# Attention sums kept as channels x tokens up to the output projection, their denominators inverted by way of DRAM, and the two output norms applied to the products

## The chip, the cores and the metric

One core of a Trainium2 chip runs the whole layer in one launch. The metric is the device time of that launch in microseconds (us). A core has a matrix engine (PE), a vector engine (DVE), a scalar engine (ACT), a general engine (POOL), and queues that issue transfers (DMA); here nearly all transfers are issued by SP, in order. SBUF is the on-chip memory, PSUM the eight accumulation banks that PE writes, DRAM the memory behind the DMAs.

## The reference

One encoder layer over 1024 tokens of width 1024, in float32:

```python
hn = rms_norm(x, norm1_g)
qa, ka, va, qb, kb, vb = split(hn @ w_in)              # A: 8 q heads, 2 kv heads; B: 8 heads; 64 channels each
out_a = softmax(rope(norm(qa)) @ rope(norm(ka)).T / 8) @ va          # dense, 4 q heads to a kv head
out_b = mixture of three dilated windows over norm(qb), norm(kb), vb # one sum over 3 patterns, one denominator
mixed = concatenate([rms_norm(out_a, outa_norm_g), rms_norm(out_b, outb_norm_g)], -1)   # 512 + 512 columns
x = x + mixed @ w_out                                  # 1024 x 1024
x = x + conv_ffn(rms_norm(x, norm2_g), w_up, conv_w, conv_b, w_down) # gate/value, width-3 conv, gelu
```

`rms_norm(y, g) = y * rsqrt(mean(y*y) + 1e-6) * g`, over the last axis.

## The kernel before

**Data.** All of SBUF is two arenas: `bigf` (float32) and `bigr` (the form that PE takes at its fast rate). A float32 product is made of three fast matmuls: a value is split into a high part (a copy into `bigr`) and a low part (value minus high part), and high x high, high x low and low x high are summed in a PSUM bank (`ps`). A copy by ACT and a subtraction by DVE make one split. A PE transpose of a `bigf` tile needs no split; in the profile it is a MATMUL `ps<-bigf`.

**Order of the work.** The code calls engine methods through a `Recorder`. It keeps every operation, works out dependences, and a planner (`price`, `simulate`) places them: PE's operations carry their place in the code as priority, those of the other engines a latest start worked out from prices; `emit` then writes each engine's queue in that planned order. So each engine runs its instructions in a fixed order, every instruction has the same source line (L462 before, L467 after the change, as order prints them), and an instruction that waits holds up whatever stands behind it on its engine. A DMA on SP also waits for the DMA eight before it, whose semaphore it shares.

**Stages.** Input projections and their norms; attention A in 16 groups `g` (128 tokens `b`, kv head `kv`; four q heads are one 512-wide tile); attention B, 8 heads of 8 steps `s` with a lag of two steps between scores (`b_s`) and sums (`b_pv`); output projection, residual and second norm; the feed-forward's two products.

**Attention A** (`a_main`). For each of 8 key tiles `kt`: scores on PE, two exponentials on ACT (one to `bigr` as the high part `ph`, one in place in PSUM), DVE subtracts them to the low part `pl`; three matmuls (`pv`) add value x probability into a bank, three key tiles behind. The bank holds 64 channels x 512 (4 heads x 128 tokens), and row 64 the denominators. `o_out` (ACT) copies the 65 rows to SBUF. `o_turn` then turns them back with four PE transposes of 65 rows, and `o_norm` (DVE) takes the reciprocal of 4 denominators per token and multiplies: tokens x channels, into the q tile that is no longer needed. The tail of a group (`pv(5..7)`, `o_out`, `o_turn`) runs inside the next.

**Attention B** (`b_pv`, `b_out`). The sums for 512 tokens (`hf` 0 or 1) lie as 65 x 512 in banks 6 and 7; the last matmuls of a head (steps 4 to 7) have the float32 weight `F_VCN` (65 columns) and appear as `ps<-bigf 128*65`. `b_out` turns and divides as in A, one step later.

**Output projection.** `x` tiles run in the order `seq(i)`. `mix_norm(i, u)` takes the RMS of 512 columns (u = 0: A, u = 1: B): an ACT square with a sum, DVE, an ACT square root, four DVE operations (`newton`), one DVE product with scale and gain. `mix_tr(i, u)` transposes the 128 x 512 result with four PE transposes, and `evac_split` makes the split operand from PSUM. `proj_out(i, u, hf)` is 12 matmuls of 512 columns, both `u` into one bank of a ring of six (`pj`). `h2_a` adds the residual, squares, norms; `h2_b` transposes for the feed-forward. `wo_load`/`wo_split` load and split the eight 128-row blocks of `w_out` through three buffers `F_WOR`; the first blocks are split in B's last head (`mixer_out_early`), which also does `mix_norm` for two tiles. `wu_load` loads `w_up` into four buffers, two of which are `F_WOR`'s.

Of the kernel before, what the change touches and what calls it, by code (L numbers as in the profile page):

```python
# [129 lines left out]
class Recorder:  # L130
# [335 lines left out]
def tile_encoder_layer(ctx, tc, x, xt, w_kv, w_in, gains, outg, norm2_g, w_out, w_up, conv,  # L466
# [471 lines left out]
    def a_main(g, prep, tail, late, plan, late_plan):  # L938
# [38 lines left out]
        return [lambda: pv(5), lambda: pv(6), lambda: pv(7), o_out, o_turn]  # L977

    def o_norm(t, step, dst, dims):
        rec = f(SM_T + 88 + 8 * (t % 2), 4)  # L980
        vec.reciprocal(rec, pp(512 * t + 64, [step, 4]))
        vec.tensor_tensor(fp(dst, *dims), pp(512 * t, [step, 4], [1, 64]), rec[:, :, None].to_broadcast([128, 4, 64]),
                          op=OP.mult)


# [190 lines left out]
    def x_load(i):  # L1176
        dma(f(F_X + 1024 * (i % 2), 1024), perm_rows(x, seq(i), D))

    def mix_norm(i, u):
        t = SM_T + 16 * (i % 2) + 8 * u  # L1180
        o = fp(q_at(1 - u, seq(i), 0), [512, 2], [1, 256])
        act(heads(f(F_JK3, 256).bitcast(BF), 2), o, AF.Square, accum_out=f(t, 1))
        vec.tensor_scalar(f(t + 1, 1), f(t, 1), 1.0 / 512, EPS, op0=OP.mult, op1=OP.add)
        act(f(t + 2, 1), f(t + 1, 1), AF.Sqrt)
        newton(f(t + 3, 1), f(t + 1, 1), f(t + 2, 1), f(t + 4, 1))
        vec.scalar_tensor_tensor(o, o, f(t + 3, 1), heads(f(F_OG + 512 * u, 512), 2), op0=OP.mult, op1=OP.mult)

    def mix_tr(i, u):
        b = next_tr()
        for k in range(4):  # L1190
            tr_f(b, k, f(q_at(1 - u, seq(i), k // 2) + 128 * (k % 2), 128))
        evac_split(xs(i) + 512 * u, b)

    def pj(i, hf):
# [607 lines left out]
```

## Time and profile before

| | us |
|---|---|
| median of 3 runs (1270.86 to 1271.05) | 1270.92 |
| the profiled execution | 1271.11 |
| its span (first to last instruction) | 1269.3 |
| TensorE clock granted, mean of the span | 1.0 of full speed |

The stages in that span: input projections to about 177 us (with the preparation of A), A to about 407, B to about 539, output projection to about 645, feed-forward to the end. In the profile a row of groups reads: engine, operation, out<-in with sizes, xcount, busy time, mean ns of one, and what ended the idle time before. A matmul's own duration includes its way through the array, so the rate is read from the distance between starts. A row of the timeline is: start, duration, engine, operation, count, and in brackets idle time and its releaser.

### The profile page before, as it was taken

The page shows a single profiled execution, that of the slowest core. Times are in us where ns is not written, and L with a number is a line of the kernel's source. Part 1 is how long each engine was busy: PE and PEld are TensorE (multiplying, and loading weights), DVE is VectorE, ACT ScalarE, POOL GpSimd, SP SyncE. Part 2 cuts the span into 40 slices and gives each one's busy share as a digit, 9 for nine tenths or more (in the row PEclk, how much of TensorE's full clock was granted, in tenths as well). Part 3 has the DMA queues.
Part 4 walks back from the last instruction along what each step waited for, and adds up shares of the span by engine and source line. Part 5 has one row for each costly group of instructions (what it writes and reads, how often), then busy time and mean ns, then how long its engine had stood idle before and what let it go on. Part 6 is the DMA issues. An engine that isn't in the chain of part 4 may idle for free.

```text
span 1269.3 us, 17891 instructions
## 1 busy us (share of the span) xinstructions
PE 1255.4 (99%) x6244; PEld 1048.8 (83%) x6244; DVE 1078.7 (85%) x1940; ACT 745.9 (59%) x1222; POOL 88.9 (7%) x92
## 2 busy tenths in 40 slices
PE   7999999999999999999999999999999999999998
PEld 7888887888888999778888888888888888888887
DVE  5988889999887888886699989999999998876664
ACT  6876479988888777763455444444444455344331
POOL 0011230020002221001120000000000000000000
PEclk9999999999999999999999999999999999999999
DMA  9242341000005445442321322333322248977862
GB/s 358 73 161 67 83 126 40 13 1 10 1 18 138 121 115 131 127 163 85 108 74 51 125 94 89 100 108 108 125 93 90 100 148 285 325 257 234 283 228 104
DMA packets 118777, 157.43 MB, mean 124 GB/s; under 512 B 50720, under 2 KB 75808, under 8 KB 117664
## 3 DMA queue, kind: packets, MB, share of 16 engines
q1 hardware_dynamic: 117392, 152.88, 37.2%
q0 software_dynamic: 1152, 3.15, 0.9%
q8 instruction: 49, 0.80, 0.3%
q10 hardware_dynamic: 144, 0.27, 0.1%
q14 instruction: 40, 0.33, 0.1%
HBM read 118.26 MB, written 33.82 MB: 120 GB/s over the span
## 4 chain that ended last, share of the span: by engine, by line
PE 93%; DVE 3%; ACT 2%; issue 1%; DMA 1%; POOL 1%; DVEq 0%; ACTq 0%; POOLq 0%
PE ps L462 93%; DVE bigf L462 2%; DVE bigr L462 1%; ACT bigr L462 1%; POOL bigf L462 0%; DMA bigf<-w_out 0%; DMA bigf<-w_kv 0%; ACT bigf L462 0%; ACT L462 0%; ACT ps L462 0%; POOL bigr L462 0%; DVEq L462 0%; ACTq L462 0%; POOLq L462 0%
## 5 line engine op out<-in xcount | busy, mean ns | idle before, releaser
L462 PE MATMUL ps<-bigr 128*128 128x512 f32 (+3 forms) x5860 | 1226.1, 369 | 8.5 <-ACT bigr L462 7.5
L462 PEld LDWEIGHTS ps<-bigr 128*128 128x128 f32 x5860 | 1010.3, 186 | 202.6 <-ACT bigr L462 11.7
L462 ACT ACTIVATE bigr<-bigf 128x512 fp32r<-128x512 f32 (+2 forms) x388 | 276.8, 727 | 350.6 <-PE ps L462 284.7
L462 DVE TENSOR_TENSOR bigr<-bigf,bigr 128x512 fp32r<-128x512 f32 (+2 forms) x354 | 283.4, 813 | 62.9 <-ACT bigr L462 58.9
L462 DVE TENSOR_TENSOR bigf<-bigf 128x512 f32<-128x512 f32 (+3 forms) x308 | 213.7, 718 | 24.0 <-DMA bigf<-w_down 12.5
L462 DVE TENSOR_TENSOR bigf<-ps,bigf 128x512 f32<-128x512 f32 (+3 forms) x260 | 174.8, 681 | 40.5 <-PE ps L462 35.1
L462 ACT ACTIVATE bigr<-ps 128x512 fp32r<-128x512 f32 x292 | 166.6, 602 | 68.7 <-PE ps L462 64.7
L462 ACT ACTIVATE bigf<-bigf 128x1024 f32<-128x1024 f32 (+6 forms) x194 | 152.1, 804 | 43.3 <-DVE bigf L462 29.0
L462 DVE SCALAR_TENSOR_TENSOR bigf<-bigf 128x255 f32<-128x255 f32 (+5 forms) x283 | 161.6, 591 | 5.3 <-ACT bigf L462 2.5
L462 DVE TENSOR_TENSOR bigr<-ps,bigr 128x512 fp32r<-128x512 f32 x188 | 127.4, 685 | 31.2 <-ACT ps L462 22.1
L462 ACT ACTIVATE ps<-ps 128x512 f32<-128x512 f32 x192 | 115.0, 600 | 12.6 <-PE ps L462 11.6
L462 ACT ACTIVATE bigf<-ps 128x512 f32<-128x512 f32 (+3 forms) x112 | 70.2, 634 | 27.5 <-DVE bigf L462 13.7
L462 DVE TENSOR_REDUCE bigf<-ps 128x1 f32<-128x512 f32 x128 | 81.5, 681 | 0.9 <-PE ps L462 0.8
L462 PE MATMUL ps<-bigf 65*128 65x65 f32 (+2 forms) x384 | 63.2, 293 | 1.3 <-DVE bigf L462 1.3
L462 POOL TENSOR_TENSOR bigr<-bigf,bigr 128x512 fp32r<-128x512 f32 x32 | 41.8, 1311 | 313.4 <-ACT bigr L462 185.8
L462 PEld LDWEIGHTS ps<-bigf 65*128 65x128 f32 (+2 forms) x384 | 43.7, 139 | 13.3 <-DVE bigf L462 2.3
L462 POOL TENSOR_TENSOR bigf<-bigf 128x256 f32<-128x256 f32 (+2 forms) x29 | 34.3, 1205 | 193.8 <-DVE bigf L462 187.4
L462 DVE CUSTOM_DVE_ANT_1 bigf<-ps,bigf 128x432 bf16<-128x432 f32 x64 | 38.5, 602 | 4.2 <-PE ps L462 2.8
L462 DVE CUSTOM_DVE_ANT_0 bigf<-ps,bigf 128x256 bf16<-128x256 f32 x64 | 26.8, 419 | 1.2 <-PE ps L462 1.2
L462 DVE TENSOR_REDUCE bigf<-bigf 128x16 f32<-128x1024 f32 x13 | 15.8, 1215 | 0.5 <-ACT bigf L462 0.5
L462 ACT ACT_TABLE_LOAD x11 | 14.1, 1283 | 1.4 <-PEq L1794 1.2
L462 POOL MEMSET bigr<- 64x512 f32 (+2 forms) x18 | 8.1, 478 | 40.3 <-PE ps L462 40.2
(17 smaller groups left out, 50.6 us busy)
## 6 DMA issues: line engine op xcount, KB each, us to landing
bigf<-w_down SPq DMA_DIRECT2D x99, 256.0 KB, 3.9
bigf<-w_up SPq DMA_DIRECT2D x44, 512.0 KB, 3.5
bigf<-gscr SPq DMA_DIRECT2D x77, 256.0 KB, 4.0
gscr<-bigf SPq DMA_DIRECT2D x33, 512.0 KB, 2.9
bigf<-w_in SPq DMA_DIRECT2D x8, 1024.0 KB, 6.8
bigf<-x SPq DMA_DIRECT2D x16, 512.0 KB, 4.6
bigf<-tmx SPq DMA_DIRECT2D x8, 672.0 KB, 4.4
bigr<-bigr SPq DMA_DIRECT2D x16, 256.0 KB, 3.3
```

Of the source, the lines that this page charges most:

```text
L462: method(*args, **kw)
```

## The change

- **A.** `o_turn` and `o_norm` go. After `o_out` two DMAs move the sums to the q tile as channels x tokens (two heads on the 128 partitions), and one DMA writes the row of 512 denominators to DRAM (`dscr`). After each second group, `inverse` reads 1024 denominators back as 128 x 8, DVE inverts them, a DMA writes them, and two DMAs read them back repeated over 64 partitions each (`F_RB`). POOL multiplies the sums by them and forms the sum of squares over the heads (`F_SS`, 128 partitions x tokens).
- For two of the eight key tiles (`kt` 0 and 4) the second exponential goes to SBUF and POOL makes `pl` from it, not DVE.
- **B.** The same with `b_out`, called from `b_pv`; `inverse` after each second head, for `hf` 0 and 1. The squares of the last pair of heads are made by ACT, the others by POOL.
- **Output projection.** No transposes of attention outputs: `mix_split` splits them in place. Instead four `square_sums` (each four PE transposes of `F_SS` and a DVE reduction) give the sums of squares per token, `mix_rms` the two roots for all 8 tiles at once. The gain goes into the rows of `w_out` in `wo_split`; the RMS factor is applied to the product in `proj_add`, so u = 0 and u = 1 have banks of their own and two additions to the residual. Three `x` buffers, not two.
- The planner's price of a reciprocal changes from `n / 0.96 + 92` to `6.2 n + 68`.

```diff
@@ Recorder.price
             if name == "reciprocal":
-                t += 24
+                t = 6.2 * n + 68
@@ a_main
         def o_out():
-            act(f(F_OT[g % 2], 512)[0:65], bank(ob)[0:65], AF.Copy)
-
-        def o_turn():
-            t = next_tr()
-            for i in range(4):
-                pe.transpose(bank(t, 65, 128 * i), f(F_OT[g % 2] + 128 * i, 128)[0:65], f(O_IDF, 65)[0:65])
-            o_norm(t, 128, q_at(1, b, kv), ([64, 4], [1, 64]))
+            o = F_OT[g % 2]
+            act(f(o, 512)[0:65], bank(ob)[0:65], AF.Copy)
+            for u in range(2):
+                dma(fp(q_at(1, b, kv), [128, 2], [1, 128])[64 * u:64 * u + 64],
+                    fp(o + 128 * u, [256, 2], [1, 128])[0:64])
+            dma(d_ap(0, b, 512 * kv, [512, 1], [1, 512]), f(o, 512)[64:65])
+            if kv:
+                inverse(b, [[0, 64], [256, 4], [1, 128]], 128)
+                o, sq = fp(q_at(1, b, 0), [512, 2], [1, 256]), F_SQ
+                gp.tensor_tensor(o, o, heads(f(F_RB, 512), 2), op=OP.mult)
+                gp.tensor_tensor(heads(f(sq, 512), 2), o, o, op=OP.mult)
...
-            act(bank(st), bank(st), AF.Exp)
-            vec.tensor_tensor(r(pl, 512), bank(st), rf(ph, 512), op=OP.subtract)
+            if kt in (0, 4) and True:
+                act(f(p, 512), bank(st), AF.Exp)
+                gp.tensor_tensor(r(pl, 512), f(p, 512), rf(ph, 512), op=OP.subtract)
+            else:
+                act(bank(st), bank(st), AF.Exp)
+                vec.tensor_tensor(r(pl, 512), bank(st), rf(ph, 512), op=OP.subtract)
...
+    def inverse(n, dims, step):
+        d = f(F_D8 + 8 * (n % 2), 8)
+        dma(d, d_ap(0, n, 0, [8, 128], [1, 8]))
+        vec.reciprocal(d, d)
+        dma(d_ap(1, n, 0, [8, 128], [1, 8]), d)
+        for u in range(2):
+            dma(f(F_RB, 512)[64 * u:64 * u + 64], d_ap(1, n, step * u, *dims))
+
+    def square_sums(u, hf):
+        t = next_tr()
+        for i in range(4):
+            tr_f(t, i, f(F_SS + 512 * hf + 128 * i, 128))
+        vec.tensor_reduce(f(F_RMS + 8 * u + 4 * hf, 4), heads(bank(t), 4), axis=AX.X, op=OP.add)
@@ b_pv, b_out
-            vec.tensor_tensor(o[0:65], bank(6 + hf)[0:65], o[0:65], op=OP.add)
+            vec.tensor_tensor(f(F_OD[hf], 512)[0:65], bank(6 + hf)[0:65], o[0:65], op=OP.add)
+            b_out(h, hf)
...
+        dma(x[64 * u:64 * u + 64], heads(f(F_OD[hf], 512), 4)[0:64])
+        dma(d_ap(0, n, 512 * u, [512, 1], [1, 512]), f(F_OD[hf], 512)[64:65])
+        if u == 0:
+            return
+        inverse(n, [[0, 64], [1, 512]], 512)
+        gp.tensor_tensor(x, x, heads(f(F_RB, 512), 4), op=OP.mult)
...
@@ output projection
+    def mix_rms(u):
+        s, v, rt, t = [f(F_RMS + 16 * i + 8 * u, 8) for i in range(4)]
+        vec.tensor_scalar(v, s, 1.0 / 512, EPS, op0=OP.mult, op1=OP.add)
+        act(rt, v, AF.Sqrt)
+        newton(s, v, rt, t)
+
+    def mix_split(i, u):
+        o, d = fp(q_at(1 - u, seq(i), 0), [512, 2], [1, 256]), xs(i) + 512 * u
+        act(heads(r(d, 512), 2), o, AF.Copy)
+        vec.tensor_tensor(heads(r(d + 1024, 512), 2), o, heads(rf(d, 512), 2), op=OP.subtract)
...
+    def proj_add(i, u):
+        for hf in range(2):
+            x = f(F_X[i % 3] + 512 * hf, 512)
+            vec.scalar_tensor_tensor(f(qab(seq(i)) + 512 * hf, 512) if u else x, bank(pj(i, u, hf)),
+                                     f(F_RMS + 8 * u + seq(i), 1), x, op0=OP.mult, op1=OP.add)
```

How the queues stand around B's end. On PE (`ps` is a PSUM bank; `bigf 65x256` is a float32 sum of B's steps 4 to 7, `bigf 128x65` a transpose of `b_out`, `bigf 128x128` one of `mix_tr`), before, from the last head's step 5 on:

```order
L462 MATMUL ps<-bigf 65x256 x2
L462 MATMUL ps<-bigr 128x512 x19
L462 MATMUL ps<-bigf 65x256 x2
L462 MATMUL ps<-bigf 128x65 x4
L462 MATMUL ps<-bigf 65x256 x2
L462 MATMUL ps<-bigr 128x512 x5
L462 MATMUL ps<-bigf 128x65 x4
L462 MATMUL ps<-bigr 128x512 x13
L462 MATMUL ps<-bigf 128x128 x4
```

The turns stand between the last sums and among the first wide matmuls of the projection. After (`bigf 128x128` is now `square_sums`, later `h2_b`):

```order
L467 MATMUL ps<-bigf 65x256 x2
L467 MATMUL ps<-bigr 128x512 x16
L467 MATMUL ps<-bigf 65x256 x4
L467 MATMUL ps<-bigr 128x512 x90
L467 MATMUL ps<-bigf 128x128 x4
L467 MATMUL ps<-bigr 128x512 x7
L467 MATMUL ps<-bigf 128x128 x4
L467 MATMUL ps<-bigr 128x512 x40
L467 MATMUL ps<-bigf 128x128 x8
```

After the last sum of B, 90 wide matmuls stand ahead of the first transposes: 8 of `proj(0, 0, 1)`, 48 of `proj` for tiles 1 and 2 with A's columns, then 24 of `proj(0, 1, ...)`, the first that read B's output, and 10 of tile 3.

On SP, the transfers of that place, before:

```order
L462 DMA bigf<-w_out 128x1024 x4
L462 DMA bigf<-x 128x1024
L462 DMA bigf<-w_out 128x1024
L462 DMA bigf<-x 128x1024
L462 DMA bigf<-w_up 128x4x256 x2
```

Nothing but loads stands there. After, from the last head's denominators for `hf` 0 (`dscr<-bigf 1x512`) to the repeated read for `hf` 1 (`bigf<-dscr 64x512`):

```order
L467 DMA dscr<-bigf 1x512
L467 DMA bigf<-bigf 64x4x128
L467 DMA bigf<-dscr 128x8
L467 DMA bigf<-x 128x1024
L467 DMA bigf<-w_out 128x1024
L467 DMA bigf<-x 128x1024
L467 DMA bigf<-w_up 128x4x256
L467 DMA dscr<-bigf 1x512
L467 DMA dscr<-bigf 128x8
L467 DMA bigf<-bigf 64x4x128
L467 DMA bigf<-w_up 128x4x256 x2
L467 DMA bigf<-dscr 64x512 x2
```

The read for `hf` 0 stands behind two loads of `w_up`, which go into the buffers of the last two `w_out` blocks and so wait for their splits.

On POOL in the middle of A, before, four gains of B's q (`128x4x256`), the constants and the splits for B's first heads (`128x8x64`) are all there is:

```order
L462 TENSOR_TENSOR bigr<-bigf,bigr 128x8x64
L462 MEMSET bigr 64x512 x4
L462 TENSOR_TENSOR bigr<-bigf,bigr 128x8x64
L462 TENSOR_TENSOR bigf<-bigf 128x4x256 x4
L462 TENSOR_TENSOR bigr<-bigf,bigr 128x8x64 x6
```

None of these rows belongs to A's probabilities. After, `pl` (`bigr<-bigf,bigr 128x512`) and the work on read-back denominators (`bigf<-bigf 128x2x256` is the product that waits for them) take turns:

```order
L467 TENSOR_TENSOR bigr<-bigf,bigr 128x512 x3
L467 TENSOR_TENSOR bigf<-bigf 128x2x256
L467 TENSOR_TENSOR bigf<-bigf 128x512
L467 TENSOR_TENSOR bigr<-bigf,bigr 128x512
L467 TENSOR_TENSOR bigf<-bigf 128x256
L467 TENSOR_TENSOR bigf<-bigf 128x128
L467 TENSOR_TENSOR bigr<-bigf,bigr 128x512 x3
```

So a `pl` now stands behind a product that waits for a transfer.

More of the change, by code (lines that the diff above doesn't have):

```diff
@@ L477, in tile_encoder_layer @@
     kvscr = dpool.tile([8, 128, 256], F32, name="kvscr")
+    dscr = dpool.tile([2, 16, 1024], F32, name="dscr")
     rscr = dpool.tile([8, 128, D], F32, name="rscr")
@@ L975, in a_main, with d_ap @@
                 pv(kt - 3)
[L977 to L983, printed above, removed]
+        return [lambda: pv(5), lambda: pv(6), lambda: pv(7), o_out]
+    def d_ap(i, n, off, *dims):
+        return bass.AP(tensor=dscr.tensor, offset=dscr.offset + 16384 * i + 1024 * n + off, ap=[list(d) for d in dims])
+    def inverse(n, dims, step):
[10 more added lines that the diff above has]
+        vec.tensor_reduce(f(F_RMS + 8 * u + 4 * hf, 4), heads(bank(t), 4), axis=AX.X, op=OP.add)
     def nat_rows(h, t):
@@ L1176, in x_load, with pj, proj @@
     def x_load(i):
[L1177 to L1194, printed above, removed]
-        return (0, 1, 2, 3, 6, 7)[(2 * i + hf) % 6]
-    def proj_out(i, u, hf):
-        b = pj(i, hf)
+        dma(f(F_X[i % 3], 1024), perm_rows(x, seq(i), D))
+    def mix_rms(u):
[7 more added lines that the diff above has]
+        vec.tensor_tensor(heads(r(d + 1024, 512), 2), o, heads(rf(d, 512), 2), op=OP.subtract)
+    def pj(i, u, hf):
+        return (0, 1, 2, 3, 6, 7)[pj_at.setdefault((i, u, hf), len(pj_at)) % 6]
+    pj_at = {}
+    def proj(i, u, hf):
+        b = pj(i, u, hf)
         for k in range(4 * u, 4 * u + 4):
@@ L1213, in h2_a @@
         o = qab(seq(i))
[L1214 to L1216 removed]
+        proj_add(i, 1)
         act(f(hn(i), 1024), f(o, 1024), AF.Square, accum_out=f(t, 1))
@@ L1386, in tile_encoder_layer @@
         if g == 11:
+            tail.append(lambda: square_sums(0, 0))
+        if g == 4:
+            dma(f(F_OG, 8), outg)
+        if g == 11:
             load_k(0)
@@ L1433, in tile_encoder_layer @@
                 load_vc(h1 + 1)
-        h1, s1 = divmod(gs - lag - 1, 8)
-        if h1 >= 0 and s1 in (5, 7):
-            b_out(h1, (s1 - 5) // 2)
+        if gs == 12:
+            square_sums(0, 1)
         if s == 7 and h < 6:
@@ L1647, in tile_encoder_layer @@
         wo_split(k)
-    x_load(0)
-    x_load(1)
-    mix_norm(0, 1)
-    mix_norm(1, 1)
-    mix_tr(0, 1)
+    for i in range(3):
+        x_load(i)
+    mix_split(2, 0)
+    proj_add(0, 0)
+    for i in range(1, 3):
+        proj(i, 0, 0)
+        proj(i, 0, 1)
+        proj_add(i, 0)
+    mix_split(0, 1)
+    mix_split(3, 0)
     for i in range(8):
         if i < 7:
-            proj_out(i + 1, 0, 0)
-            mix_tr(i + 1, 1)
-            proj_out(i + 1, 0, 1)
+            mix_split(i + 1, 1)
+        if i < 4:
+            mix_split(i + 4, 0)
+        proj(i, 1, 0)
         if 0 < i < 7:
             h2_b(i - 1, 0)
-        proj_out(i, 1, 0)
+        proj(i, 1, 1)
         if 0 < i < 7:
             h2_b(i - 1, 1)
-        proj_out(i, 1, 1)
-        if i < 6:
-            mix_norm(i + 2, 0)
-            mix_tr(i + 2, 0)
-            mix_norm(i + 2, 1)
-        h2_a(i)
-        if i < 6:
-            x_load(i + 2)
+        if i == 0:
+            square_sums(1, 0)
+            square_sums(1, 1)
+            mix_rms(1)
+        h2_a(i)
+        if i < 5:
+            x_load(i + 3)
+            for hf in range(2):
+                proj(i + 3, 0, hf)
+            proj_add(i + 3, 0)
         if i == 6:
```

68 lines of the change are left out of this document (39 added, 29 removed).

## Prediction

> **What bounds the kernel now.** I read the page first: busy shares, then the chain that ended last.
>
> ```profile
> PE 1255.4 (99%) x6244; PEld 1048.8 (83%) x6244; DVE 1078.7 (85%) x1940; ACT 745.9 (59%) x1222; POOL 88.9 (7%) x92
> PE 93%; DVE 3%; ACT 2%; issue 1%; DMA 1%; POOL 1%; DVEq 0%; ACTq 0%; POOLq 0%
> ```
>
> PE is busy 99% of the span and is 93% of the chain. A share is an average, so next come the stages: A from 211 to 393 us, B to 516, the way from B into the output projection, and the projection.
>
> ```profile
> 211.00:393.00 182.00, 182.00 (x943) 150.37 (x942) 164.42 (x328) 162.14 (x310) 13.49 (x7) 1.00 0.06 17
> 407.00:516.00 109.00, 109.00 (x831) 99.03 (x830) 89.79 (x290) 80.89 (x151) 23.12 (x21) 1.00 0.49 125
> 516.00:545.00 29.00, 26.90 (x161) 21.84 (x160) 24.99 (x54) 22.02 (x36) 0.00 (x0) 1.00 0.51 168
> 545.00:640.00 95.00, 95.00 (x470) 77.85 (x470) 70.96 (x178) 46.77 (x111) 12.34 (x9) 1.00 0.33 108
> ```
>
> The columns are stretch, length, then busy time of PE, PEld, DVE, ACT, POOL, the clock, DMA share and GB/s. PE has no gap in A, in B or in the projection; only between them, at 516 to 545 us, does it idle, for 29.00 - 26.90 = 2.1 us. So a PE instruction taken away in these stages is time taken from the end, as long as the other engines keep up, and the question is what the instructions are worth. A matmul's own duration contains its way through the array, so I take distances between starts. First the pace: the chain's longest piece is the feed-forward.
>
> ```profile
> 642.74 620.41 PE ps L462 x2735
> ```
>
> 620.41 / 2735 = 0.2268 us for one wide matmul.
>
> **The change, part by part.** The turns of `mix_tr` (16 groups of four transposes 128 x 128) go; the timeline of PE in the projection prices one:
>
> ```profile
> 600.08 0.60 PE L462 MATMUL ps<-bigf 128*128 128x128 f32 x4
> 600.43 3.00 PE L462 MATMUL ps<-bigr 128*128 128x512 f32 x12
> 603.26 1.03 PE L462 MATMUL ps<-bigf 128*128 128x128 f32 x8
> ```
>
> From 600.08 to 600.43 the four take 0.35 us. The 12 wide matmuls behind them take 603.26 - 600.43 = 2.83 us where the pace gives 12 x 0.2268 = 2.72: another 0.11 us for going back to the other form. 0.46 us a group: 16 groups are -7.4 us. The four groups of `square_sums` are the same kind: +1.8 us.
>
> The turns of `o_turn` and `b_out` are 32 groups of four of 65 rows.
>
> ```profile
> 306.45 0.41 PE L462 MATMUL ps<-bigf 65*128 65x65 f32 x4
> 306.67 2.53 PE L462 MATMUL ps<-bigr 128*128 128x512 f32 x10
> 330.49 0.41 PE L462 MATMUL ps<-bigf 65*128 65x65 f32 x4
> 412.30 0.41 PE L462 MATMUL ps<-bigf 65*128 65x65 f32 x4
> 412.51 2.68 PE L462 MATMUL ps<-bigr 128*128 128x144 f32 x19
> ```
>
> The third row is the turn two groups on: a group of A takes 24.04 / 2 = 12.0 us. The four transposes take 0.22 us in A and 0.21 in B until the next matmul starts; what it loses at the change of form I take as 0.11 again in A, where a wide one follows: 16 x 0.33 = 5.3 us. In B narrower ones follow, so I take the middle of 0.22 and 0.33: 16 x 0.27 = 4.3. Together -9.6 us; the ends are 32 x 0.22 = 7.0 and 32 x 0.33 = 10.6. The projections' and scores' matmuls keep their number.
>
> The idle time between B and the projection has three pieces that I can name:
>
> ```profile
> 518.74 1.28 ACT L462 ACT_TABLE_LOAD   x1
> 520.68 0.51 PE L462 MATMUL ps<-bigr 128*128 128x256 f32 x2 [0.63 <-ACT bigr L462]
> 524.73 0.66 PE L462 MATMUL ps<-bigf 128*128 128x128 f32 x4 [0.83 <-DVE bigf L462]
> 544.09 0.66 PE L462 MATMUL ps<-bigf 128*128 128x128 f32 x4 [0.47 <-DVE bigf L462]
> ```
>
> The last two rows are transposes of `mix_tr` that wait for `mix_norm`'s product. The second row waits for an exponential that comes late because the square roots of `mix_norm` change ACT's function table amid the last head (the first row, 1.28 us, is one such load). All three go with `mix_norm`: -1.9 us. `mix_rms(0)` still needs one root there, one change to and fro where before there were two.
>
> On PE that is -7.4 + 1.8 - 9.6 - 1.9 = -17.1 us. Now what is added beside PE.
>
> Vector and scalar work first:
>
> ```profile
> L462 DVE RECIPROCAL bigf<-ps 128x4 f32<-128x4 f32 x32 | 5.6, 176 | 3.8 <-PE ps L462 3.8
> L462 DVE TENSOR_TENSOR bigf<-ps,bigf 128x256 f32<-128x256 f32 x32 | 13.5, 422 | 1.3
> L462 DVE TENSOR_TENSOR bigr<-ps,bigr 128x512 fp32r<-128x512 f32 x188 | 127.4, 685 | 31.2 <-ACT ps L462 22.1 <-ACT bigf L462 5.1 <-ACT bigr L462 2.9
> L462 DVE SCALAR_TENSOR_TENSOR bigf<-bigf 128x512 f32<-128x512 f32 x16 | 12.0, 749 | 0.3
> L462 ACT ACTIVATE bigf<-bigf 128x512 bf16<-128x512 f32 x16 | 10.0, 624 | 0.7 <-DVE bigf L462 0.5
> ```
>
> In A, DVE loses two subtractions of 0.685 us and one division of 0.176 + 0.422 per group, some 2.0 us of its 10.9 (164.42 us over 182 at 12.0 us a group); ACT stays. B's DVE loses the 0.6 us too. In the projection the 16 products of 0.749 and the 16 ACT squares go, and 16 more additions with a factor (0.75 each) come: DVE stays near its 71 us of 95. None of these reaches PE: 0 us.
>
> POOL gets 32 subtractions and the products of the sums.
>
> ```profile
> L462 POOL TENSOR_TENSOR bigr<-bigf,bigr 128x512 fp32r<-128x512 f32 x32 | 41.8, 1311 | 313.4 <-ACT bigr L462 185.8 <-DVE bigf L462 78.6 <-PE ps L462 46.4
> L462 POOL TENSOR_TENSOR bigf<-bigf 128x256 f32<-128x256 f32 x20 | 16.7, 864 | 30.9 <-DVE bigf L462 24.5 <-ACT bigf L462 6.4
> L462 POOL TENSOR_TENSOR bigf<-bigf 128x512 f32<-128x512 f32 x4 | 5.6, 1407 | 2.2 <-DVE bigf L462 2.2
> ```
>
> For two groups of A: 4 x 1.31 + 2 x 1.41 + 0.86 + half of that for 128 columns = 9.3 us of 24. There is room; what matters is order. A `pl` may stand behind a product that waits for the read-back. The round trip is a write, a read, the reciprocal, a write, a read. Nearest rows (KB each, us to landing):
>
> ```profile
> kscr<-bigf SPq DMA_DIRECT2D x16, 128.0 KB, 2.2
> bigf<-kscr SPq DMA_DIRECT2D x8, 256.0 KB, 2.7
> bigf<-vscr SPq DMA_DIRECT2D x32, 64.0 KB, 4.8
> ```
>
> 2.2 + 2.7 + 0.2 + 2.2 + 2.7 = 10.0 us, or 14 where reads queue as those of `vscr` do; two groups last 24, so the buffers are free in time. A late `pl` is needed three key tiles on: 3 x 12.0 / 8 = 4.5 us, less its own 1.31, leaves 3.2 us of cover. Up to that a read-back that is late for its place costs nothing. I put 0.5 us for A and 0.5 for B, where POOL's splits have several steps of cover; the ends are 0 and 2 each.
>
> Does POOL slow DVE? Two windows of the timeline, one in A, one in the projection:
>
> ```profile
> 253.29 2.40 POOL L462 TENSOR_TENSOR bigf<-bigf 128x1024 f32<-128x1024 f32 x1 [55.03 <-DVE bigf L462]
> 254.47 1.28 DVE L462 TENSOR_REDUCE bigf<-ps 128x1 f32<-128x512 f32 x2
> 621.94 2.38 DVE L462 TENSOR_TENSOR bigr<-bigf,bigr 128x512 fp32r<-128x512 f32 x2 [0.25 <-PE ps L462]
> 622.43 3.04 POOL L462 TENSOR_TENSOR bigr<-bigf,bigr 128x512 fp32r<-128x512 f32 x2 [19.03 <-PE ps L462]
> ```
>
> Beside a busy POOL two DVE instructions that read PSUM took 1.28 us, 0.64 each, no longer than elsewhere; two with both inputs in SBUF took 2.38, 1.19 each. Nearly all of DVE's work in A and B reads PSUM, so the sum has 0 here. [...]
>
> **B's end** is where the new chain can end last. Count from T, the end of the last sum. PE then has 8 + 48 wide matmuls, 56 x 0.2268 = 12.7 us, before `proj(0, 1, 0)` reads `hf` 0 of B, and 97 and four transposes, 22.4 us, before the last `square_sums`. The read of `hf` 0's denominators is behind `w_up` on SP, which waits for the last split of `w_out`.
>
> ```profile
> 534.36 4.45 DMA bigf<-w_out
> 538.83 1.06 ACT bigr L462
> 547.41 1.50 SPq L462 DMA_DIRECT2D bigf<-w_up  x2
> L462 DVE SCALAR_TENSOR_TENSOR bigf<-bigf 128x1024 f32<-128x1024 f32 x8 | 10.3, 1285 | 0.3
> L462 DVE TENSOR_REDUCE bigf<-ps 128x1 f32<-128x512 f32 x128 | 81.5, 681 | 0.9 <-PE ps L462 0.8
> L462 ACT ACTIVATE bigf<-bigf 128x1024 f32<-128x1024 f32 x95 | 107.9, 1138 | 34.2 <-DVE bigf L462 21.9 <-DMA gscr<-bigf 10.8 <-ACT bigr L462 0.8
> ```
>
> With the last `w_out` issued at T: 4.45 landing + 1.06 copy + 1.29 low part + 1.50 for issuing two `w_up` + 2.7 read + 1.41 POOL + 0.62 ACT = 13.0 us, 0.3 us late. The ends: 0 if the load goes out 1 us earlier, 2.4 if the read takes 4.8 behind `w_up`. I take 1.0. `hf` 1 goes on from 8.3 + 0.8: read 2.7, reciprocal 0.2, write 2.2, read 2.7 + 0.8 for issues, POOL 1.41, ACT square 0.62, addition 0.7: 20.4 against 22.4. From there to `h2_b` of the first tile lie the reduction 0.68, a table load 1.28 and a root of about 0.2, two additions 1.50, the square 1.14, another root, some ten small DVE operations of about 0.17 for both, and the norm 1.29: 8.0 us against 40 x 0.2268 = 9.1. I put 0.5 for this.
>
> Sum: -17.1 + 0.5 + 0.5 + 1.0 + 0.5 = -14.6. Against the profiled execution's 1271.1 that is 1256.5; the median of the runs lies 0.2 below that execution, which I neglect.
>
> **The rivals.**
> - *B's end is not covered.* The last read-backs queue behind 2 MB of `x`, `w_out` and `w_up`, each of `hf` 1's three hops takes 4.8 where I have 2.7, 2.2 and 2.7: 6.8 us later, less 2.0 of cover, +4.8: 1261. For: 168 GB/s at a DMA share of 0.51 there already. Against: small transfers elsewhere land in 2.2 to 2.7.
> - *PE's slots come back as waits.* ACT (162.14 of 182) or DVE set A's pace as soon as PE is relieved, and A's and B's 9.6 us are not seen: 1266. Against: ACT would be at 92% of A's new length and DVE is relieved.
> - *The lock.* Each of the projection's 16 subtractions loses the 0.5 us by which the SBUF pair was slower, all on the path: +8, 1264.5. Against: DVE has 24 us to spare there and POOL works in 12 of 95.
> - *Slower: POOL's queue.* In A a product waiting for its read-back holds the `pl` behind it. Eight read-backs; the 17.1 us are gone when each is late for its place by 3.2 + 17.1 / 8 = 5.3 us. At 6.5 us late: 8 x 3.3 = +26, 1281. For: the wait is in the POOL queue, and SP's own waits are in the way of each hop. Against: a 14 us round trip is only 4 above the usual one.
> - *No change:* the first two together, 4.8 + 9.6 = 14.4 us: 1271, within the 0.2% or 2.5 us that a measurement of this kernel can tell at best.
>
> **How the numbers follow.** Forecast 0.60, B's end 0.15, slots 0.06, lock 0.05, no change 0.05, POOL's queue 0.09. Faster: 0.60 + 0.15 + 0.06 + 0.05 = 0.86. The forecast's own range is 1253 (turns at their upper price, -18.1, and no new wait) to 1260 (the upper ends of the four waits that I put in). The range reaches to the slots at 1266 and, below, two under the first end, since 7% of the chain is not PE and DVE is relieved at the start of A: 1251 to 1267.
>
> **What would show it.** PE's transposes: no group of 65 rows, 16 + 64 of 128 x 128 left. A's groups 0.3 us closer. No idle of PE behind `mix_norm`; if there is one behind ACT or DVE at `proj(0, 1, 0)` or at the last `square_sums`, its length is the price of B's end. PE waiting for POOL in A, eight times, would make the prediction wrong.

## The result, and the profile after

| | before | after |
|---|---|---|
| median, us (runs) | 1270.89 (6: 1270.65 to 1271.19) | 1261.59 (6: 1259.00 to 1262.62) |
| ratio, 95% interval | | 0.9924 (0.9912 to 0.9937) |
| profiled execution, its span | 1271.11, 1269.3 | 1259.00, 1257.2 |
| granted clock, mean of the span | 1.0 | 0.997; in the other runs 0.995 to 0.996 |

Faster by 0.76% by the ratio, and by 9.3 us by the medians, where the prediction had 14.6. The profiled execution of after is its fastest, 2.6 us under the median. The clock in the last row will matter. First the page of after, then PE's groups by form (the two float32 ones).

```profile
PE 1239.5 (99%) x6068; PEld 1036.2 (82%) x6068; DVE 1052.2 (84%) x1796; ACT 732.3 (58%) x1176; POOL 184.1 (15%) x174
PEclk9999999999998999999999999999999999999999
```

```profile
L467 PE MATMUL ps<-bigf 128*65 128x256 f32 x128 | 33.3, 381 | 0.0
L467 PE MATMUL ps<-bigf 128*128 128x128 f32 x80 | 11.7, 273 | 0.1
```

PE has 6244 - 6068 = 176 instructions fewer: 128 transposes of 65 rows and 64 - 16 of 128 x 128. All that was to go has gone. But in the row of the clock (tenths of full speed, 40 slices) the thirteenth digit is an 8 where before all were 9. That slice is A's end. Windows of after: A, the end of A in two pieces, and the way from B into the projection.

```profile
190.00:380.00 190.00, 189.65 (x918) 153.74 (x917) 158.66 (x293) 174.59 (x330) 78.88 (x69) 1.00 0.13 32
385.00:395.00 10.00, 8.55 (x62) 7.27 (x60) 3.13 (x8) 8.81 (x17) 2.51 (x2) 1.00 0.64 181
395.60:402.40 6.80, 6.33 (x27) 5.89 (x28) 5.72 (x23) 2.29 (x4) 0.38 (x1) 0.51 0.00 0
520.00:555.00 35.00, 33.30 (x158) 26.52 (x157) 27.92 (x40) 14.54 (x24) 12.74 (x8) 1.00 0.65 204
```

Inside A PE has no gap worth naming (189.65 of 190), though POOL is busy 78.9 us there and ACT 174.59 (92%). Between A and B it idles, and then runs 6.8 us at a clock of 0.51. Three points of the program give a table of what each stage became; they are starts of PE instructions in the traces (the first and last float32 sum of B, and the feed-forward's first product), and the last row is the last PE instruction.

| start, us | before | after | difference | of the stage that ends here | by the prediction's terms |
|---|---|---|---|---|---|
| first float32 sum of B | 402.19 | 403.51 | +1.3 | +1.3 | -4.4 |
| last float32 sum of B | 538.79 | 531.85 | -6.9 | -8.3 | -5.7 |
| feed-forward's first product | 641.55 | 629.61 | -11.9 | -5.0 | -4.5 |
| last PE instruction | 1264.79 | 1252.77 | -12.0 | -0.1 | 0 |

(The last column: -5.3 + 0.5 and one group of `square_sums` for A; -4.3 - 0.63 - 0.83 + 0.5, another group of `square_sums` and two of `mix_tr` for B, in whose last head those two stood and waited; the rest for the projection.) A, with the borders on both sides, lost 5.7 us against the forecast, and B won 2.6. Three places need a look.

**The border from A to B.** Rows of after: the chain, SP, DVE, PE; then SP and DVE of before.

```profile
387.99 5.93 DMA bigf<-tmx
...
384.57 1.25 SPq L467 DMA_DIRECT2D bigf<-bigf  x2
385.88 0.44 SPq L467 DMA_DIRECT2D dscr<-bigf  x1
387.32 0.48 SPq L467 DMA_DIRECT2D bigr<-bigr  x1
387.99 0.44 SPq L467 DMA_DIRECT2D bigf<-tmx  x1
...
393.94 0.61 DVE L467 CUSTOM_DVE_ANT_1 bigf<-ps,bigf 128x432 bf16<-128x432 f32 x1 [2.73 <-DMA bigf<-tmx]
...
394.62 1.27 PE L467 MATMUL ps<-bigr 128*128 128x144 f32 x4 [1.12 <-DVE bigf L467]
396.36 7.31 PE L467 MATMUL ps<-bigr 128*128 128x512 f32 x33 [0.47 <-DVE bigf L467]
```

```profile
385.92 3.98 SPq L462 DMA_DIRECT2D bigf<-tmx  x2
394.40 0.61 DVE L462 CUSTOM_DVE_ANT_1 bigf<-ps,bigf 128x432 bf16<-128x432 f32 x1 [1.15 <-DMA bigf<-tmx]
```

The table `tmx` that B's second head needs is loaded into `F_TMX[1]`, at `O_F + 4960`. A's staging tiles `F_OT` lie at `O_F + 4960` and `O_F + 5472`, inside it. Before, the load had to wait until PE had turned the last sums. It was the second of the two `tmx`, issued at 389.55, 0.6 us after ACT's copy of the last group (`o_out`, ended at 388.96); DVE waited 1.15 us for it and PE not at all. Now it has to wait until the two moves and the write out of `F_OT` have landed (387.24 in the trace), and a move ahead of it on SP (`bigr<-bigr`) holds it until ACT is done at 387.79. So it goes out at 387.99, 3.4 us after `o_out` (384.54): the copy is 4.4 us earlier than before, the load only 1.6. It lands 5.93 us later, DVE stands 2.73 us, PE 1.12 + 0.47. The prediction has no line on this border.

**The start of A.** After: PE, then the chain; behind them the chain of before.

```profile
171.43 4.91 PE L467 MATMUL ps<-bigr 128*128 128x512 f32 x30 [2.84 <-DVE bigr L467]
...
170.77 0.61 DVE bigr L467
```

```profile
171.36 0.61 DVE bigr L462
```

PE stands 2.84 us (3.00 by the starts: the row of a wide matmul is 392 ns long on average, and the next starts 227 after it). Before, the same place had gaps of 0.19 and 0.47 (0.35 and 0.63 by the starts). What waits is a wide matmul of the input projections, for a low part of 512 columns that DVE makes. Ahead of that part stand two additions on A's keys, and they wait for POOL, which is done at 168.27 (before, at 168.85). DVE is done with it no later than before (171.38 against 171.97); PE is there earlier. Up to those additions DVE has made 82 such low parts where before it had made 83, and one feeds 12 wide matmuls. The order of PE went with it: the 16 transposes of A's first keys (`ps<-bigr 128x128 x16`), which come eight wide matmuls behind the wait, stood behind 575 wide matmuls and now stand behind 564.

**B's end**, after: PE, the chain, SP, POOL.

```profile
548.92 5.78 PE L467 MATMUL ps<-bigr 128*128 128x512 f32 x24 [1.70 <-ACT bigr L467]
...
535.19 7.17 DMA dscr<-bigf
...
538.93 2.32 SPq L467 DMA_DIRECT2D bigf<-w_up  x2
542.44 1.75 SPq L467 DMA_DIRECT2D bigf<-dscr  x3
...
546.94 1.27 POOL L467 TENSOR_TENSOR bigf<-bigf 128x512 f32<-128x512 f32 x1 [10.27 <-DMA bigf<-dscr]
```

This is the wait that the prediction put at 1.0: the read of `hf` 0 goes out at 542.44, and `proj(0, 1, 0)` waits 1.70 us (1.86 by the starts). The read stands behind the two `w_up`, as forecast, but these are issued by 541.25. What ends last ahead of it is the write of the inverted denominators, issued at 535.19 and landed at 542.37. The prediction's sum for `hf` 0 has no write.

### The profile page after: what moved, and what is told of

The parts are those of the page before. It is cut to its first block, busy times and chain, and to the rows that moved or that the text cites. A ratio compares the mean times of both kernels' runs of the same rounds, so it can differ in the third digit from the quotient of the medians.

```text
span 1257.2 us, 17689 instructions
## 1 busy us (share of the span) xinstructions
PE 1239.5 (99%) x6068; PEld 1036.2 (82%) x6068; DVE 1052.2 (84%) x1796; ACT 732.3 (58%) x1176; POOL 184.1 (15%) x174
## 4 chain that ended last, share of the span: by engine, by line
PE 92%; DMA 2%; ACT 2%; DVE 1%; issue 1%; POOL 1%; SPq 0%; POOLq 0%; ACTq 0%
PE ps L467 92%; DVE bigf L467 1%; DMA bigf<-dscr 1%; DMA dscr<-bigf 1%; ACT bigr L467 1%; POOL bigf L467 1%; DMA bigf<-tmx 0%; DVE bigr L467 0%; ACT ps L467 0%; DMA bigf<-w_kv 0%; ACT L467 0%; ACT bigf L467 0%; SPq L467 0%; POOL bigr L467 0%; POOLq L467 0%
## 5 line engine op out<-in xcount | busy, mean ns | idle before, releaser
L467 DVE TENSOR_TENSOR bigf<-bigf 128x512 f32<-128x512 f32 (+4 forms) x296 | 214.1, 746 | 22.0 <-DMA bigf<-w_down 12.5
L467 ACT ACTIVATE bigr<-ps 128x512 fp32r<-128x512 f32 (+1 forms) x276 | 157.1, 599 | 45.2 <-PE ps L467 41.9
L467 ACT ACTIVATE bigf<-bigf 128x1024 f32<-128x1024 f32 (+5 forms) x166 | 141.9, 870 | 55.8 <-DVE bigf L467 37.7
L467 DVE TENSOR_TENSOR bigf<-ps,bigf 128x512 f32<-128x512 f32 (+2 forms) x212 | 149.9, 719 | 27.6 <-PE ps L467 22.8
L467 DVE SCALAR_TENSOR_TENSOR bigf<-bigf 128x255 f32<-128x255 f32 (+4 forms) x239 | 146.7, 632 | 5.9 <-ACT bigf L467 2.9
L467 DVE TENSOR_TENSOR bigr<-ps,bigr 128x512 fp32r<-128x512 f32 x140 | 96.3, 688 | 32.5 <-ACT ps L467 28.2
L467 POOL TENSOR_TENSOR bigr<-bigf,bigr 128x512 fp32r<-128x512 f32 x64 | 84.1, 1319 | 236.4 <-ACT bigr L467 127.9
L467 POOL TENSOR_TENSOR bigf<-bigf 128x512 f32<-128x512 f32 (+3 forms) x79 | 87.9, 1121 | 167.3 <-DVE bigf L467 114.6
L467 DVE TENSOR_REDUCE bigf<-ps 128x1 f32<-128x512 f32 (+1 forms) x132 | 84.3, 681 | 12.0 <-PE ps L467 12.0
L467 PE MATMUL ps<-bigf 128*65 128x256 f32 (+1 forms) x208 | 45.1, 340 | 0.1
L467 DVE SCALAR_TENSOR_TENSOR bigr<-bigf,bigr 128x256 fp32r<-128x256 f32 (+1 forms) x16 | 14.6, 936 | 0.5 <-ACT bigr L467 0.4
```

Of the source, the lines that this page charges most:

```text
L467: method(*args, **kw)
```

## The experiments

They were timed in three sets, in which the kernel before had medians of 1270.97, 1271.2 and 1271.25 us. An edit that changes a dependence or a price also lets the planner order the instructions around it anew; a run shows both together.

**Staging tiles elsewhere** (`e1_ot_moved`).

```diff
-F_OT = (O_F + 4960, O_F + 5472)
+F_OT = (O_F + 2560, O_F + 3072)
```

> One edit to the changed kernel: the staging tiles of A's sums (F_OT) lie where B's F_OD lies later, no longer inside the buffer that the second head's table tmx is loaded into. Theory (border): in the changed kernel that load has to wait for the moves out of F_OT, is issued at 387.99 us, lands 5.93 us later, DVE waits 2.73 us for it, PE's matmuls come apart between 391 and 396 us, and from 395.6 us the trace shows the PE clock at half for 6.83 us. Without the overlap the load goes out early: no such gap, no half clock, mean granted clock 1.0 again, span 4 to 7 us shorter than the 1257.2 of the profiled execution, 1251 to 1254, and the runs agree within 1 us. Rival (ACT): at the end of A, ACT's exponentials set the pace (384 to 388 us in the chain), the table only ends last by chance: gap and half clock stay, at most 1 us is won. Rival (load): the half clock comes from PE's denser work, not from the gap: the gap goes, the half clock stays somewhere, 1254 to 1256.

Measured: 1255.95 us (1254.37 to 1257.35), ratio 0.9882 (0.9868 to 0.9895), 5.6 under after. The border is gone: the load of the table now goes out at 183 us, at the start of A. PE in this kernel:

```profile
383.74 12.44 PE L467 MATMUL ps<-bigr 128*128 128x512 f32 x95
```

One piece with no wait, at full clock (the two stretches at half clock further down make up this kernel's mean clock of 0.997). The first float32 sum of B starts at 399.04, 4.5 us earlier than in after, although the start of A lost 1.7 us more here (below). Without the overlap of the two buffers nothing of the border's cost is left. At B's end a part was lost again: windows of this kernel there.

```profile
538.00:546.80 8.80, 6.02 (x24) 4.19 (x24) 6.79 (x13) 1.97 (x4) 1.26 (x1) 1.00 0.59 172
546.80:550.20 3.40, 3.40 (x10) 2.63 (x9) 3.11 (x5) 0.75 (x2) 0.87 (x1) 0.52 0.28 77
```

PE idles 8.80 - 6.02 = 2.8 us (the starts give gaps of 1.05 and 2.05) and then runs a stretch of 3.4 us at half clock. At the start of A stands another, at a clock of 0.51 from 171.4 to 174.8 us.

**`w_up` behind the read-backs** (`e2_wup_behind`): the planner gets the last read-backs as predecessors of the first four `w_up` loads.

```diff
+            if j < 2:
+                rec.behind.append((len(rec.ops) - 1, rec.last_reads))
```

> One edit to the changed kernel: the planner may place the first four loads of w_up only behind the last read-backs of the denominators, so on SP no load that waits for the last split of w_out stands ahead of the repeated read for hf 0. Theory (B's end): PE's idle 1.70 us at 548.92 us (first projection with B's columns, behind POOL's product and ACT's split) comes from that order, since the read could only be issued at 542.44 us. It goes: 1.5 to 2.5 us less, with the border of A and B as before. Rival (transfers): the read-back chain itself is too long (write 3.0, read 2.6, write 7.2, read 4.0 us in the chain): part of the idle stays, 0 to 1 us less. Rival (later): w_up lands too late for the feed-forward, a new wait of 1 us or more there.

Measured: 1263.2 us (1261.62 to 1265.5), 0.9941 (0.9929 to 0.9954): no gain. The chain and SP of this kernel:

```profile
536.94 6.25 DMA bigf<-bigf
...
543.21 0.33 SPq L471 DMA_DIRECT2D bigf<-x  x1
543.99 1.12 SPq L471 DMA_DIRECT2D bigf<-dscr  x2
```

Another load has taken the place of `w_up`: the third `x` tile goes into `F_X[2]`, which shares its place with `F_OD`; it waits for the move of `hf` 1 out of there, 6.25 us, and the read-back stands behind it. `w_up` was one of two.

**Both** (`e3_both`).

> Both edits. If border and B's end are separate waits on one chain, the gains add: 1257.2 - 5.5 - 2 = about 1250 in span, 1251 to 1253 in time, 1.5% below the kernel before. If the second is hidden by the first (or the other way), no better than the better of the two.

Measured: 1256.93 us (1256.19 to 1257.87), 0.989 (0.9876 to 0.9904): no gain over the moved tiles alone. The gap at B's end is 2.66 us, and the chain's 434 matmuls behind it take 92.51 us where they take 91.03 in `e2_wup_behind`; the mean clock of the profiled execution is 0.997, as in the moved tiles.

**A's turns put back** (`e4_turns_a`, on the moved tiles): 16 groups of four 65-row transposes into a bank that nobody reads.

```diff
+        def turn():
+            t = next_tr()
+            for i in range(4):
+                pe.transpose(bank(t, 65, 128 * i), f(F_OT[g % 2] + 128 * i, 128)[0:65], f(O_IDF, 65)[0:65])
-        return [lambda: pv(5), lambda: pv(6), lambda: pv(7), o_out]
+        return [lambda: pv(5), lambda: pv(6), lambda: pv(7), o_out, turn]
```

> To be read against the kernel with F_OT moved: its A gets the 16 groups of four PE transposes of 65 rows back, at the end of each group, into a bank of the ring that nothing reads; nothing else is put back. What the prediction gave A for them, 16 x 0.33 = 5.3 us: the span grows by 4.5 to 5.5 us. Rival (slots): A's pace is set by ACT (162 of 182 us busy) and PE's slots were free: under 2 us.

Measured: 1259.4 us (1258.16 to 1263.13), 0.9915 (0.99 to 0.993). From the 769th matmul (162.5 us in the moved tiles, 163.2 here) to B's first float32 sum it is 241.8 us against 236.5: 5.3 us for 16 groups, 0.33 each, as forecast. The medians differ by 3.5 and not 5.3; in the profiled executions the projection took 4.4 us less here, since B's end had one gap of 0.63 us; the mean clock is 0.998 where the moved tiles have 0.997.

**B's turns put back** (`e5_turns_b`, on the moved tiles): the same four lines at the head of `b_out`.

> The kernel with the staging tiles moved, plus 16 groups of four 65-row transposes put back into B (their bank is read by nobody). The prediction priced them at 0.27 us a group, 4.3 in all: 1260.3 us. After's trace has each head of B 0.9 us shorter with two groups gone, 0.45 a group, which gives 7.2: 1263.2 us, with 7.2 us more between the first and the last float32 sum of B. Between: 1260.0 to 1263.5. Rival (B got shorter for another reason, such as the bank ring of B having fewer users): under 4 us more between those sums.

Measured: 1260.65 us (1260.09 to 1260.81), 0.9913 (0.9898 to 0.9928). Between the first and the last float32 sum of B lie 134.36 us against 127.84: 6.5 us, 0.41 a group. The median rose by less (4.7); B's end again had only one gap, of 0.66 us. One group in the timeline:

```profile
422.21 0.46 PE L467 MATMUL ps<-bigf 65*128 65x65 f32 x4
422.48 0.95 PE L467 MATMUL ps<-bigr 128*128 128x128 f32 x9
```

0.27 us pass until the next matmul starts. That is all the prediction had for a group. The other 0.14 is a difference, not a row: the change of form may be in it, and the bank of the ring that the four take (the rival) is not told apart from it.

**All low parts by DVE** (`e6_pl_dve`, on the moved tiles).

```diff
-            if kt in (0, 4) and True:
+            if False:
```

> The kernel with the staging tiles moved, with all low parts of A's probabilities made by DVE again (32 subtractions of 128x512 back from POOL). DVE's share in A rises from 158.7 of 190 us by some 28 x 0.7 to about 94%. Theory (PE sets A's pace and neither vector engine is late): 1256 us, 1255 to 1257. Rival 1 (DVE then runs late in A): 1258 us or more, with PE waiting for DVE in A. Rival 2 (POOL's subtractions hold up its normalising, and with it the queue of moves): 1 to 3 us faster, below 1255.

Measured: 1256.31 us (1255.32 to 1258.26), 0.9877 (0.9861 to 0.9894): no difference. A in this kernel:

```profile
190.00:380.00 190.00, 189.70 (x918) 153.84 (x917) 172.50 (x321) 172.84 (x328) 37.15 (x36) 1.00 0.14 33
```

POOL 37 us, DVE 172.5 (91%), and PE as full as before (189.70 us of 190, 189.66 in the moved tiles). Neither POOL's queue nor DVE sets A's pace; that part of the change is worth nothing here.

**Both loads behind the read-backs** (`e7_reads_first`, on the moved tiles): as `e2_wup_behind`, and for the `x` tiles from the third on.

```diff
+        if i >= 2:
+            rec.behind.append((len(rec.ops) - 1, [p for p in rec.last_reads if p < len(rec.ops) - 1]))
```

> The kernel with the staging tiles moved (1255.95 us median) plus two holds: the first four w_up loads and the third x tile's load are placed behind B's last read-backs. Theory (B's end waits only because SP stands on those loads ahead of the read-backs): the wait ahead of the output projection's first u = 1 product falls from the 1.05 + 2.05 us with 3.41 us of half clock in the moved-staging kernel's trace to under 1 us and no half clock; 3.1 - 0.7 + 1.7 = about 4 us faster, so 1252 us (1251 to 1254). Rival (the two DRAM round trips and the move between partitions are themselves longer than the cover): the wait stays over 2 us and the time stays at 1255 to 1257 us.

Measured: 1255.76 us (1255.74 to 1258.61), 0.9881 (0.9866 to 0.9896): the median of the moved tiles. In the profiled executions B's last sum to the feed-forward takes 98.88 us against 100.96; the theory had 4 us. SP, PE and POOL of this kernel:

```profile
529.74 0.24 SPq L471 DMA_DIRECT2D dscr<-bigf  x1
530.03 0.64 SPq L471 DMA_DIRECT2D bigf<-bigf  x1
530.73 0.59 SPq L471 DMA_DIRECT2D dscr<-bigf  x1
535.06 3.18 SPq L471 DMA_DIRECT2D bigf<-dscr  x3
538.35 0.52 SPq L471 DMA_DIRECT2D dscr<-bigf  x1
541.88 1.09 SPq L471 DMA_DIRECT2D bigf<-dscr  x2
...
542.57 5.79 PE L471 MATMUL ps<-bigr 128*128 128x512 f32 x24 [2.53 <-ACT bigr L471]
540.60 1.26 POOL L471 TENSOR_TENSOR bigf<-bigf 128x512 f32<-128x512 f32 x1 [8.39 <-DMA bigf<-dscr]
```

No load stands between them now, and SP still waits. The first of the three reads at 535.06 is `hf` 1's and waits for the write of 529.74 (`dscr<-bigf`, one row of 2 KB), 5.3 us. The other two are the read-back of `hf` 0. They wait for the write of 530.73 (128 rows of 32 bytes), whose last part lands at 536.86, 6.1 us after its issue; POOL's product, ACT's copy and then PE wait for them. The read-back of `hf` 1 at 541.88 waits for POOL (SP 1.2 us): both halves are read into the one `F_RB`, and POOL needs it for `hf` 0 until 541.86. The write ahead of that read, of 538.35, had landed at 540.69. The rival was right: the wait stays over 2 us (2.53). The round trip of `hf` 0 outlasts the cover, and `hf` 1 then queues for the buffer. The half clock at this place did go (mean clock 0.999, in the moved tiles 0.997).

**The old price of a reciprocal** (`e8_old_price`, on the kernel with both holds).

```diff
-                t = 6.2 * n + 68
+                t += 24
```

> The previous kernel (both holds) with the planner's old price of a reciprocal, n / 0.96 + 92. Only the order near A's start changes: the 16 transposes of A's first keys stand after 575 wide matmuls again, as before the change, instead of after 564. Theory (the 3.0 us gap at 168 us and the 3.41 us of half clock behind it come from that order alone): gap 3.0 -> 1.4 us and no half clock (1.7 us), so 3.3 us less than the kernel with both holds, 1249 us (1248 to 1250). Rival (the keys are late because of DVE and POOL, and PE waits as long wherever its transposes stand): within 0.7 us of it.

Measured: 1251.51 us (1250.78 to 1251.87), 0.9841 (0.9827 to 0.9856), 4.3 under the same kernel with the new price. PE at the start of A:

```profile
171.99 4.13 PE L471 MATMUL ps<-bigr 128*128 128x512 f32 x29 [0.17 <-DVE bigr L471]
176.63 1.65 PE L471 MATMUL ps<-bigr 128*128 128x512 f32 x6 [0.51 <-ACT bigr L471]
```

The wait is 0.17 + 0.51 and the clock stays at 1.0. B's first float32 sum starts 3.6 us earlier (395.85 against 399.49). But the expectation has the cause too narrow. The transposes stand behind 575 wide matmuls again, and DVE has its 83rd low part ahead of the additions on the keys again; from 81 us on DVE, ACT, POOL and SP too run in another order than in the kernel with the new price. The run shows what the price costs; that it goes by the low part on DVE is read from the rows above, and no run moved that alone. So the 3.6 us came with the edit of one price that no part of the new computation needs. (B takes 0.7 us longer here than in `e7_reads_first`: in its last head PE waits in small pieces for splits of DVE.)

**The turns of `mix_tr` put back** (`e9_turns_mix`, on `e8_old_price`): four 128 x 128 transposes at each `mix_split`.

```diff
+        t = next_tr()
+        for k in range(4):
+            tr_f(t, k, f(q_at(1 - u, seq(i), k // 2) + 128 * (k % 2), 128))
```

> The kernel with moved staging tiles, both holds and the old price (1251.5 us), plus 16 groups of four 128x128 transposes, one at each split of the output projection's inputs, as the kernel before had them; their bank is read by nobody. The prediction's term (16 x 0.46): 7.4 us slower, 1258.9 us (1258 to 1260), and the stretch from B's last float32 sum to the feed-forward's first product 7 us longer. Rival (the turns stood in idle time of the projection, so their removal gave little): 1252 to 1256. A third reading (in a place where the input is still waited for, at B's end, 2 or 3 of the groups are free): about 6 us, 1257.5.

Measured: 1258.91 us (1258.07 to 1259.34), 0.9903 (0.9889 to 0.9916): 7.4 us by the medians. Between the two profiled executions it is 5.8 us from B's first float32 sum to the feed-forward, with 0.7 us less idle time at B's end (gaps of 1.83 and 0.28 in the base, 0.53 and 0.87 here): 6.5 us, 0.41 a group. The term lies between 6.5 and 7.4.

**More cover** (`e10_cover`, on `e8_old_price`): the products of the fourth tile with A's columns go ahead of the first with B's.

```diff
+    for hf in range(2):
+        proj(3, 0, hf)
     mix_split(0, 1)
-    mix_split(3, 0)
```

> The same base (1251.5 us) with 24 more wide matmuls (the fourth tile's u = 0 products, 5.4 us) ahead of the output projection's first u = 1 product. Theory (what is left at B's end is the latency of two DRAM round trips and a product, against the cover of the u = 0 products): the 1.8 us gap goes, 1249.7 us (1249.2 to 1250.6). Rival (the bank ring or the third x tile then makes the wait, since two banks are held 5 us longer): the gap comes back within the next two tiles and the time stays at 1251 to 1253.

Measured: 1251.23 us (1250.95 to 1251.52), 0.9843 (0.983 to 0.9857): the rival. PE in this kernel:

```profile
524.18 22.16 PE L471 MATMUL ps<-bigr 128*128 128x512 f32 x96
546.96 5.71 PE L471 MATMUL ps<-bigr 128*128 128x512 f32 x24
553.74 4.15 PE L471 MATMUL ps<-bigr 128*128 128x512 f32 x17 [1.06 <-DVE bigf L471]
558.40 1.09 PE L471 MATMUL ps<-bigf 128*128 128x128 f32 x8 [0.51 <-DVE bigf L471]
```

96 wide matmuls run through, and `proj(0, 1, 0)` no longer waits; a little later PE waits 1.06 and 0.51 us for DVE (1.22 and 0.67 by the starts, together 1.89 where it was 1.83). The first ends when DVE's `proj_add` (552.93) frees a bank; it stands behind the reductions and roots of B's sums, and these behind seven subtractions (545.88 to 550.18). The wait has moved to DVE and the bank ring, and was not made shorter. This kernel and `e8_old_price` are the fastest of the study; they cannot be told apart.

## Why the prediction was right, and where it was not

- **The direction and the main mechanism held:** PE paces A, B and the projection (busy in after 189.65 of 190 us, 107.87 of 108 from 407 us on, 79.50 of 79.50 from 549.5 us on), and the turns taken from it were time taken from the end: put back, they cost 5.3, 6.5 and 6.5 to 7.4 us.
- **`mix_tr`, -7.4:** measured 6.5 to 7.4.
- **65-row turns of A, -5.3:** measured 5.3.
- **Of B, -4.3:** mis-sized; measured 6.5. The step that failed is "narrower ones follow, so I take the middle of 0.22 and 0.33": a group put back into B costs 0.41, more than the 0.33 of A, which was the stated upper end. Which part of it is the change of form is not shown.
- **Waits inside A, 0.5:** 0.35 us at most (189.65 of 190 us busy).
- **Idle at B's end, -1.9 + 1.0:** the place was right, the size 1.7 to 1.9 instead of 1.0, so the gain there is nought. The reason given, the read of `hf` 0 behind `w_up`, was not the one that ended last: the sum for `hf` 0 leaves out the write of its inverted denominators, which landed 7.2 us after its issue in after and 6.1 in `e7_reads_first`, with `w_up` and the third `x` tile out of the way. For a write the prediction had 2.2 us, from the row of `kscr`; `hf` 1's in `e7_reads_first`, with no loads in its way, took 2.3. And it has no term for the one `F_RB`, for which `hf` 1 waits.
- **What was missing:** the borders of A. "PE has no gap in A, in B or in the projection" was read from windows that leave out 160 to 211 and 393 to 407 us, and the sum has no term there. The border cost 5.6 us by the medians, half clock included (`e1_ot_moved`), the start of A 3.6 to 4.3 (`e8_old_price`, with all that the price reorders; in after's own profiled execution, without half clock at this place, about 2). Together they are 8.4 us of after's profiled execution: from the 769th matmul to B's first sum it takes 241.4 us, and 233.0 in `e8_old_price`, which has neither. The total lies 5 us above the forecast and not 8 because an overlooked loss and gains priced too low partly made up for each other. That much of the nearness is luck.

Taken together in the profiled executions, from before to `e8_old_price`: 6.3 us in A (of which turns 5.3), 8.0 in B (turns 6.5, the waits of the last head 0.63 and 0.83, two groups of `mix_tr` 0.8, less 0.4 for a group of `square_sums` and 0.7 for the new waits for splits: 7.7 of it), 4.8 in the projection: 19.1 of the 19.3 us by which the span is shorter. Without the two accidents at A's borders the change is worth more than forecast (that kernel also has both holds, which by the medians gave nothing).

Of the rivals, *POOL's queue* is refuted by A's window and by `e6_pl_dve`; *slots come back as waits* by `e4_turns_a`. *The lock* (0.5 us lost by each subtraction, from the SBUF pair of 1.19 us each beside a busy POOL in before): in after the projection's subtractions took

```profile
542.68 2.48 DVE L467 TENSOR_TENSOR bigr<-bigf,bigr 128x512 fp32r<-128x512 f32 x4
```

0.62 us each, with POOL idle until 546.94. Three later ones ran beside a busy POOL (552.25 to 553.87, 603.56 to 606.12) and took longer (two at 552.03 took 2.39 together, one at 605.27 took 1.40); why is not shown. But PE had no gap from 549.5 to 629 us; no loss. *B's end is not covered* happened in kind, at 1.7 to 1.9 us instead of 4.8 more.

## What to carry to other kernels

When a tile's last reader changes from an engine to a DMA, look up everything that shares its address: the tile can be held longer (here its next load went out 3.4 us after the copy into it and not 0.6). In a round trip through DRAM count every write, with the loads that go out ahead of it (here 7.2 and 6.1 us to landing behind loads, 2.3 without them), and the buffer that two round trips share (here 1.2 us of waiting in `e7_reads_first`). Read the borders between stages as closely as the stages; here 8.4 us of what the change freed was lost there. When a planner sets the order, compare the queues also where the change has no business, and leave its prices alone unless the change needs them.

## What the runs showed of the hardware

**Half clock followed gaps in PE's stream.** From 12.0 to 1268.1 us, past its last PE instruction, before runs at full clock. After has one stretch at half clock ahead of its last PE instruction, 6.83 us from 395.72 on (0.50 from 395.72 to 402.55); the moved tiles have two of 3.4 us (0.51 from 171.4 to 174.8, 0.52 from 546.8 to 550.2); `e8_old_price` has none (1.00 in each of four windows from 160 to 622 us, mean 1.0). In after's stretch matmuls of 256 columns in a row start 213 to 214 ns apart, where elsewhere it is 120, and behind the wide one at 400.95 us the next starts after 426 and not 227. From these distances the cost of a stretch is estimated at about half its length, 1.7 us for 3.4 and 3.4 for 6.83; 1.7 us in 1257 is 0.0014 of the mean clock. This is the likely cause of after's spread of 3.6 us (mean clocks 0.995 to 0.997) against 0.5 before, read from the mean clocks alone.

The clock records of after are 385.71 us long at full clock, 6.83 at half and 853.33 at full, that of before 1256.11 at full: 113, 2, 250 and 368 times 3.413, half of 6.83. The two stretches of `e1_ot_moved` begin 375.4 us apart, 110 times. Idle time (what a gap between starts has over the usual distance, from 0.1 us on) is counted here in steps of 3.413 us from the first record on. In after the step ahead of the half clock (392.31 to 395.72 us) has 2.3 us, in gaps of up to 1.28. The 3.00 us at the start of A lie across two steps, 2.02 in the first and about 1 in the second, and the clock behind them is 1.00 (171.0 to 174.4 us). The step with the gap at B's end (545.91 to 549.32) has 1.97, and the clock behind it is 1.00 too (549.4 to 552.8). No step of before has over 1.05.

Other kernels at these two places: at the start of A `e1_ot_moved` and `e7_reads_first` have half clock where after has none (0.51 from 171.4 to 174.8 and from 172.5 to 175.9 us). At B's end gaps of 1.05 and 2.05 us in `e1_ot_moved` had half clock behind them, while one of 2.69 in `e7_reads_first` had none (the mean clock of 0.999 leaves room for the stretch at the start of A alone). So the length of a gap does not settle it by itself in these runs. No experiment set the length or the position of a gap on its own, and a limit is not shown.

**Two small writes to DRAM landed late behind loads (5.3 and 6.1 us), and one as small without them after 2.3.** In `e7_reads_first` the row of 2 KB issued at 529.74 landed after 5.3 us and the 4 KB in 128 pieces of 32 bytes issued at 530.73 after 6.1; both went out behind loads of `x` and `w_out`. The same 4 KB for `hf` 1, issued at 538.35, landed at 540.69, after 2.3 us, when the DMA engines had little else to do. (Landing is the last update of the transfer's semaphore in the trace.) Their busy tenths in this kernel from 524 to 545 us, in 40 slices of 0.53 us:

```profile
DMA  9889721100799899999952110005351000002699
```

From the 12th to the 20th slice (529.8 to 534.5 us) the engines are full, and the first two writes land just behind that; the third goes out in the 28th. A write of 128 KB (`kscr<-bigf`) took 2.2 us in the kernel before. The move of one head's sums to other partitions, 6.25 us in `e2_wup_behind`, went out beside loads.
